# Forgetting attention on one core: the two f16 halves of every third probability tile both on GpSimd, and a scale folded into the ones column

## The chip, the cores and the metric

The kernel runs on one core of a Trainium2 chip. The metric is the device time of one execution in microseconds (us). A core has five engines that run their own queues and meet through semaphores: TensorE (PE: matrix multiply; PEld is its weight load), VectorE (DVE), ScalarE (ACT), GpSimd (POOL) and SyncE (SP), which here issues the transfers.

## The reference

One layer of a hybrid mixer over 2048 tokens of width 1024. A normalised input is projected and split over three groups of heads: a gated linear recurrence, a pooling mixer, and attention with a forget gate in 8 heads of 64. The change touches only the third:

```python
def _forgetting_attention(q, k, v, log_f):
    B, T, H, D = q.shape
    c = jnp.cumsum(log_f, axis=1).transpose(0, 2, 1)
    scale = D ** -0.5
    outs = []
    for i in range(T // Q_BLOCK):
        q0, q1 = i * Q_BLOCK, (i + 1) * Q_BLOCK
        s = jnp.einsum('bqhd,bkhd->bhqk', q[:, q0:q1], k[:, :q1]).astype(jnp.float32) * scale
        mask = (q0 + jnp.arange(Q_BLOCK))[:, None] >= jnp.arange(q1)[None, :]
        bias = jnp.where(mask, c[:, :, q0:q1, None] - c[:, :, None, :q1], 0.0)
        p = jax.nn.softmax(jnp.where(mask, s + bias, MASK_VALUE), axis=-1)
        outs.append(jnp.einsum('bhqk,bkhd->bqhd', p.astype(v.dtype), v[:, :q1]))
    return jnp.concatenate(outs, axis=1)
```

Its output is multiplied by a SiLU gate, joined with the other two groups and mapped by one output projection.

## The kernel before

**Stages.** Up to about 670 us the kernel makes all projections, the recurrence and the pooling mixer. From there to about 1170 us it runs the attention, with the gate projection (tiles pgc), then the output projection (tiles y) fed in between as filler matmuls. After that come the last output rows.

**Numbers in f16 pairs.** Every factor of a matmul is kept as a high and a low f16 half. So a probability tile is made as pf (f32), ph (its f16 rounding) and pl (pf minus ph in f16), and each value product takes three matmuls into the bank o: ph by the values' high half with a ones column beside it (65 columns), ph by the low half (64), pl by the high half and the ones column (65). The ones column gives the row sum, as column 64 of o. It is set once, by a GpSimd memset on the value tile Vt (L686).

**The attention's loops.** Queries come in 4 groups g of 512, and for each group the 8 heads h follow; a head sweeps 4g+4 key tiles j of 128. That makes 320 steps (g, h, j). A step is one call of `scores` (L1002): matmuls into a score bank st (two banks), an exponential on ScalarE into pf (L1019; three buffers), then ph and pl, by a counter k that goes 0, 1, 2 over the steps:

- k = 0: GpSimd copies pf to ph (L1021), VectorE subtracts to pl (L1024).
- k = 1: ScalarE makes ph by a second exponential (L1023), GpSimd subtracts to pl (L1024).
- k = 2: ScalarE makes ph (L1023), VectorE subtracts to pl (L1024).

`values` (L1027) issues the value products four steps later (LAG). At a head's last step VectorE takes the reciprocal of the row sums (rl, L1045), multiplies it by a constant (L1046) and scales o by it into oc (L1048). The bank o is single: the next head's first value product waits until L1048 has read it.

**Row maxima.** A third stream, `max_steps` (L956), runs ahead by about one head: TensorE makes scores into the banks mx (three), VectorE reduces each to a column of M (L979 for a full tile, L976 for one on the diagonal), and the head's maxima become Mf (L985, L986) and an f16 pair Mc (L988, L989). TensorE transposes Mc (mt, L995), and ScalarE copies it into QB (L997), without which no score of that head can be made.

**Order.** The kernel's text interleaves these streams, and a scheduler then fixes the order of the instructions on each engine when the kernel is built, from its own estimate of when each could start. At run time every engine works through its list in that order, so an instruction that has to wait holds all that stand behind it. y is drained by VectorE (L1086, L1095), with a small GpSimd power (L1091) between; a finished pair of heads is gated (L1051) and split (L409 on ScalarE, L411 on VectorE).

Of the kernel before, what the change touches and what calls it, by code (L numbers as in the profile page):

```python
# [16 lines left out]
ALU = mybir.AluOpType  # L17
# [14 lines left out]
INV = 1.0 / (SW * SH)  # L32
SM = 16.0
SV = 16.0
# [20 lines left out]
def kernel(  # L55
# [7 lines left out]
    V, S, G, PE = nc.vector, nc.scalar, nc.gpsimd, nc.tensor  # L63
# [357 lines left out]
    def store_tm(src, slot, g):  # L421
        for v, dst in zip(split(spool, src, 1.0, f"mx{slot}_{g}_"), (mh_d, ml_d)):
            nc.sync.dma_start(dst[g * GT:(g + 1) * GT, slot * P:(slot + 1) * P].rearrange("(t p) c -> p t c", p=P),
                              v.rearrange("p (t c) -> p t c", t=4))
# [258 lines left out]

    vp = ctx.enter_context(tc.tile_pool(name="vp", bufs=1, side="right", reuse_waits="tile"))
    Vt = vp.tile([P, NT, 8, 130], F16, tag="Vt", name="Vt")
    G.memset(Vt[:, :, :, 64:65], SV)  # L686

    negq = vp.tile([P, GT], BF16, tag="negq", name="negq")
    G.memset(negq, 0.0)
# [219 lines left out]
    def bank(tag, name):  # L909
        return psB.tile([P, 512], F32, tag=tag, name=name, bufs=BANKS[tag])  # L910
# [91 lines left out]
    def scores(n, g, h, j):  # L1002
        i = n % NQ
        q0 = max(0, j - 4 * g)
        off = q0 * P
        diag = j >= 4 * g
        c, jj = j // 4, j % 4
        st = bank("st", f"st{g}_{h}_{j}")
        PE.matmul(st[:, off:], K2[c][:, h, jj * P:(jj + 1) * P], QQs[i][:, off:], start=True, stop=False)  # L1009
        PE.matmul(st[:, off:], KA[c][:68, h, jj * P:(jj + 1) * P], QBs[i][:68, off:], start=False, stop=not diag)  # L1010
        if diag:
            PE.matmul(st[:, off:off + P], idb, negk, start=False, stop=True)
        pf = wk.tile([P, GT], F32, tag="pf", name=f"pf{g}_{h}_{j}", bufs=3)
        ph = wk.tile([P, GT], F16, tag="ph", name=f"ph{g}_{h}_{j}", bufs=6)
        pl = wk.tile([P, GT], F16, tag="pl", name=f"pl{g}_{h}_{j}", bufs=5)
        bias = biasg[:, g, 8 * j + h:8 * j + h + 1]
        k = state["step"] % 3
        state["step"] += 1
        S.activation(pf[:, off:], st[:, off:], AF.Exp, bias=bias, scale=0.125)  # L1019
        if k == 0:  # L1020
            G.tensor_scalar(ph[:, off:], pf[:, off:], 1.0, 1.0, op0=ALU.mult, op1=ALU.mult)  # L1021
        else:
            S.activation(ph[:, off:], st[:, off:], AF.Exp, bias=bias, scale=0.125)  # L1023
        (G if k == 1 else V).tensor_tensor(pl[:, off:], pf[:, off:], ph[:, off:], op=ALU.subtract)  # L1024
        return ph, pl, q0

    def values(n, g, h, j, ph, pl, q0):  # L1027
        if j == 0:
            state[n] = bank("o", f"o{g}_{h}")
        po = state[n]  # L1030
        pov = po[:, :260].rearrange("p (q d) -> p q d", d=65)
        for qi in range(q0, 4):
            qs = slice(qi * P, (qi + 1) * P)
            PE.matmul(pov[:, qi, :], ph[:, qs], Vt[:, j, h, 0:65], start=(j == 0 and qi == 0), stop=False, skip_group_check=True)  # L1034
            PE.matmul(pov[:, qi, 0:64], ph[:, qs], Vt[:, j, h, 65:129], start=False, stop=False, skip_group_check=True)  # L1035
            PE.matmul(pov[:, qi, :], pl[:, qs], Vt[:, j, h, 0:65], start=False, stop=(j == 4 * g + qi), skip_group_check=True)  # L1036
        if j < 4 * g + 3:
            return
        if h % 2 == 0:
            state["oc"] = wk.tile([P, 4, P], F32, tag="oc", name=f"oc{g}_{h}", bufs=2)  # L1040
            state["gt"] = wk.tile([P, 4, P], F32, tag="gt", name=f"gtl{g}_{h}", bufs=1)
            nc.sync.dma_start(state["gt"], gc_d[g * GT:(g + 1) * GT, (h // 2) * P:(h // 2 + 1) * P].rearrange("(q p) c -> p q c", p=P))
        oc, gt = state["oc"], state["gt"]
        rl = wk.tile([P, 4], F32, tag="rl", name=f"rl{g}_{h}", bufs=2)
        V.reciprocal(rl, pov[:, :, 64])  # L1045
        V.tensor_scalar(rl, rl, SM * INV * 0.5, None, op0=ALU.mult)  # L1046
        cs = slice(64 * (h % 2), 64 * (h % 2) + 64)
        V.tensor_tensor(oc[:, :, cs], pov[:, :, 0:64], rl.unsqueeze(2).to_broadcast([P, 4, 64]), op=ALU.mult)  # L1048
        del state[n]
        if h % 2 == 1:  # L1050
            V.tensor_tensor(oc, oc, gt, op=ALU.mult)  # L1051
            store_tm(oc.rearrange("p q c -> p (q c)"), 2 + h // 2, g)
# [73 lines left out]
    def pop_value():  # L1126
        a = pend.pop(0)
        values(*a)
        n, g, h, j = a[:4]
        if h == 7 and j == 4 * g + 3:  # L1130
            state["closing"] = (state["step"] + 10, g)
# [20 lines left out]
    for n, (g, h) in enumerate(order):  # L1152
        for j in range(4 * g + 4):
            while deadlines and deadlines[0] <= step:
                deadlines.pop(0)
                next(maxs, None)
            pend.append((n, g, h, j) + scores(n, g, h, j))
            if "closing" in state and state["step"] >= state["closing"][0]:
                state["done"] = state.pop("closing")[1] + 1
            credit += RATE  # L1160
            while credit > 0.0:
                cost = next(fill, None)
                if cost is None:
                    credit = 0.0
                else:
                    credit -= cost
            if len(pend) > LAG:
                pop_value()
            step += 1
# [33 lines left out]
```

## Time and profile before

| what | value |
|---|---|
| median of 3 runs | 1251.9 us (1248.07 to 1254.1) |
| the profiled execution | 1248.18 us, span 1246.4 us |
| granted TensorE clock | 0.987 |
| busy share: PE, DVE, ACT, POOL | 94%, 65%, 49%, 32% |

The span runs from the first to the last instruction; 1.8 us of the execution lie around it. Matmuls overlap in the records, so a busy TensorE is not one at its peak, but a hole in its row is a real wait. The lines that the prediction rests on stand with it.

### The profile page before, as it was taken

To read this page: it belongs to the slowest core of one execution; us is meant where nothing else is said; L and a number is where in the kernel's file an instruction comes from. 1 tells how busy PE (TensorE), PEld (TensorE's weight loads), DVE (VectorE), ACT (ScalarE), POOL (GpSimd) and SP (SyncE) were. 2 spreads that over 40 slices of the span, in tenths; PEclk is the share of its full clock that TensorE was granted. 3 is DMA by queue.
4 is the path that set the end of the run, shared out by engine and by line. 5 is a ranking of instruction groups with operands and counts; after the bars stand their busy time and mean duration, and the time that the engine had idled before them with its cause. 6 is when DMAs were issued, how large, how long until landed. Compare 5 with 4: busy or idle time off the path is not lost.

```text
span 1246.4 us, 25487 instructions
## 1 busy us (share of the span) xinstructions
PE 1170.5 (94%) x9949; PEld 749.9 (60%) x9949; DVE 812.2 (65%) x1736; ACT 609.5 (49%) x1176; POOL 403.7 (32%) x500
## 2 busy tenths in 40 slices
PE   5877999999999999999999999999989899999998
PEld 3445667655644588884447767755555555555544
DVE  5787878887433243214364799788788888888522
ACT  5756444553121222212122677667767676777611
POOL 2645555553130020002230223234334343434400
PEclk9988999999999999999999999999999999999999
DMA  9646100113175232101112343285223222321263
GB/s 226 184 115 170 44 17 18 52 35 93 43 183 142 71 107 71 35 2 43 26 51 70 89 140 110 69 178 127 67 64 85 68 78 79 65 51 38 80 162 104
DMA packets 168137, 107.56 MB, mean 86 GB/s; under 512 B 95824, under 2 KB 159568, under 8 KB 168016
## 3 DMA queue, kind: packets, MB, share of 16 engines
q1 hardware_dynamic: 166976, 105.92, 32.2%
q8 instruction: 78, 1.28, 0.4%
q14 instruction: 43, 0.35, 0.1%
q10 hardware_dynamic: 1040, 0.00, 0.0%
HBM read 59.62 MB, written 31.59 MB: 73 GB/s over the span
## 4 chain that ended last, share of the span: by engine, by line
PE 62%; DVE 19%; ACT 6%; issue 5%; POOL 4%; DMA 4%; SPq 0%; POOLq 0%; DVEq 0%; ACTq 0%
PE y L1078 11%; PE pq L183 7%; PE pv L194 6%; PE pgc L194 5%; PE pu L183 3%; PE st L1009 3%; PE st L1010 3%; PE pgb L183 3%; PE pk L183 3%; DVE pl L1024 3%; PE mx L973 3%; DVE M L979 3%; PE o L1034 2%; PE o L1035 2%; PE pf L183 2%
## 5 line engine op out<-in xcount | busy, mean ns | idle before, releaser
L1019 ACT ACTIVATE pf<-st,biasg 128x512 f32<-128x512 f32 (+1 forms) x320 | 199.6, 625 | 93.9 <-PE st L1010 53.2
L194 PEld LDWEIGHTS <-hTh 128*128 128x128 f16 x1536 | 151.0, 99 | 44.3 <-DMA hTh<-xh 16.1
L1024 DVE TENSOR_TENSOR pl<-pf,ph 128x512 f16<-128x512 f32 (+1 forms) x213 | 139.9, 658 | 42.4 <-POOL ph L1021 24.8
L1024 POOL TENSOR_TENSOR pl<-pf,ph 128x512 f16<-128x512 f32 (+2 forms) x107 | 114.2, 1067 | 147.7 <-ACT ph L1023 137.6
L979 DVE TENSOR_REDUCE M<-mx 128x1 f32<-128x512 f32 x192 | 129.2, 682 | 9.4 <-PE mx L973 8.5
L1023 ACT ACTIVATE ph<-st,biasg 128x512 f16<-128x512 f32 (+2 forms) x213 | 131.4, 617 | 2.1 <-PE o L1036 2.1
L1034 PE MATMUL o<-Vt,ph 128*128 128x65 f16 x1088 | 129.7, 193 | 2.8 <-DVE oc L1048 2.4
L1035 PE MATMUL o<-Vt,ph 128*128 128x64 f16 x1088 | 130.2, 195 | 0.0
L1036 PE MATMUL o<-Vt,pl 128*128 128x65 f16 x1088 | 129.2, 192 | 0.0
L1021 POOL TENSOR_SCALAR ph<-pf 128x512 f16<-128x512 f32 (+1 forms) x107 | 66.0, 617 | 192.4 <-ACT pf L1019 130.8
L1034 PEld LDWEIGHTS <-ph 128*128 128x128 f16 x1088 | 102.6, 96 | 34.5 <-issue 5.5
L1009 PE MATMUL st<-QQ,K 128*128 128x512 f16 (+1 forms) x320 | 111.5, 349 | 5.6 <-ACT ph L1023 5.0
L1035 PEld LDWEIGHTS <-ph 128*128 128x128 f16 x1088 | 101.8, 97 | 24.5 <-issue 1.1
L1036 PEld LDWEIGHTS <-pl 128*128 128x128 f16 x1088 | 102.3, 99 | 0.4
L1078 PE MATMUL y<-woh,mh 128*128 128x512 f16 (+2 forms) x264 | 98.2, 373 | 0.0
L1078 PE MATMUL y<-woh,ml 128*128 128x512 f16 (+2 forms) x264 | 98.0, 373 | 0.0
L1078 PE MATMUL y<-wol,mh 128*128 128x512 f16 (+2 forms) x264 | 98.0, 373 | 0.0
L973 PE MATMUL mx<-KA,QM 68*128 68x512 f16 (+1 forms) x224 | 79.5, 358 | 5.7 <-DVE M L979 4.1
L194 PEld LDWEIGHTS <-hTl 128*128 128x128 f16 x768 | 75.5, 98 | 9.9
L1010 PE MATMUL st<-QB,KA 68*128 68x512 f16 x224 | 80.1, 358 | 0.0
L1078 PEld LDWEIGHTS <-mh 128*128 128x128 f16 x528 | 49.4, 98 | 50.4 <-issue 0.7
L976 DVE CUSTOM_DVE_ANT_0 mx<-mx,negq 128x128 f32<-128x128 f32 (+3 forms) x128 | 62.3, 492 | 12.0 <-PE mx L973 11.5
(327 smaller groups left out, 2691.1 us busy)
## 6 DMA issues: line engine op xcount, KB each, us to landing
xt<-in_x_dram SPq DMA_DIRECT2D x16, 512.0 KB, 4.4
xr<-in_x_dram SPq DMA_DIRECT2D x16, 512.0 KB, 4.5
out_dram<-yt SPq DMA_DIRECT2D x15, 512.0 KB, 3.1
QQ<-qh_d SPq DMA_DIRECT2D x64, 64.0 KB, 2.3
wo<-in_w_out_dram SPq DMA_DIRECT2D x16, 256.0 KB, 3.0
gc_d<-gtc SPq DMA_DIRECT2D x32, 128.0 KB, 2.0
gtl<-gc_d SPq DMA_DIRECT2D x16, 256.0 KB, 2.9
wst_q<-in_w_in_dram SPq DMA_DIRECT2D x12, 256.0 KB, 2.9
```

Of the source, the lines that this page charges most:

```text
L183: PE.matmul(ps, a[:, k, c0:c0 + P], b[:, k, :], start=i == 0, stop=i == 3 * KC - 1)
L194: PE.matmul(ps, a[:, k, :], b[:, k, c0:c0 + n], start=i == 0, stop=i == 3 * KC - 1)
L979: V.tensor_reduce(dst, mx[:, :w], op=ALU.max, axis=AX.X)
L1009: PE.matmul(st[:, off:], K2[c][:, h, jj * P:(jj + 1) * P], QQs[i][:, off:], start=True, stop=False)
L1010: PE.matmul(st[:, off:], KA[c][:68, h, jj * P:(jj + 1) * P], QBs[i][:68, off:], start=False, stop=not diag)
L1019: S.activation(pf[:, off:], st[:, off:], AF.Exp, bias=bias, scale=0.125)
L1023: S.activation(ph[:, off:], st[:, off:], AF.Exp, bias=bias, scale=0.125)
L1024: (G if k == 1 else V).tensor_tensor(pl[:, off:], pf[:, off:], ph[:, off:], op=ALU.subtract)
L1034: PE.matmul(pov[:, qi, :], ph[:, qs], Vt[:, j, h, 0:65], start=(j == 0 and qi == 0), stop=False, skip_group_check=True)
L1035: PE.matmul(pov[:, qi, 0:64], ph[:, qs], Vt[:, j, h, 65:129], start=False, stop=False, skip_group_check=True)
L1036: PE.matmul(pov[:, qi, :], pl[:, qs], Vt[:, j, h, 0:65], start=False, stop=(j == 4 * g + qi), skip_group_check=True)
L1078: PE.matmul(py, a[:, k, :], b[:, k, cs], start=i == 0, stop=i == 3 * KC - 1)
```

## The change

At k = 0 the subtraction moves from VectorE to GpSimd, so GpSimd makes ph and then pl of the same step. At k = 1 it moves from GpSimd to VectorE. Over three steps each engine has as many instructions as before. The constant of L1046 goes: its reciprocal is now in the ones column, so the row sum comes out already scaled, and lines behind it are numbered one lower (L1048 becomes L1047, L1095 becomes L1094).

```diff
     Vt = vp.tile([P, NT, 8, 130], F16, tag="Vt", name="Vt")
-    G.memset(Vt[:, :, :, 64:65], SV)
+    G.memset(Vt[:, :, :, 64:65], SV / (SM * INV * 0.5))
...
         else:
             S.activation(ph[:, off:], st[:, off:], AF.Exp, bias=bias, scale=0.125)
-        (G if k == 1 else V).tensor_tensor(pl[:, off:], pf[:, off:], ph[:, off:], op=ALU.subtract)
+        (G if k == 0 else V).tensor_tensor(pl[:, off:], pf[:, off:], ph[:, off:], op=ALU.subtract)
         return ph, pl, q0
...
         V.reciprocal(rl, pov[:, :, 64])
-        V.tensor_scalar(rl, rl, SM * INV * 0.5, None, op0=ALU.mult)
         cs = slice(64 * (h % 2), 64 * (h % 2) + 64)
```

With other instructions to place, the scheduler also sets some others in another order. Names below are tile_head_key tile with the buffer's number behind.

VectorE in group g = 2, from the last maxima of head 5 (Mf_5) to its pair Mc_5, before:

```order
L985 TENSOR_REDUCE Mf_5_10948<-M_5_10947 128x4
L1024 TENSOR_TENSOR pl_4_6_11266<-pf_4_6_11264,ph_4_6_11265 128x512
L411 TENSOR_TENSOR mx_2_l<-oc_2_10852,mx_2_h 128x512
L986 TENSOR_SCALAR Mf_5_10948<-Mf_5_10948,cref_74 128x4
L979 TENSOR_REDUCE M_6_11289<-mx_6_0_0_11291 128x1
L988 CAST Mc_5_11258<-Mf_5_10948 128x4
L979 TENSOR_REDUCE M_6_11289<-mx_6_0_1_11315 128x1
L989 TENSOR_TENSOR Mc_5_11258<-Mf_5_10948,Mc_5_11258 128x4
```

and after:

```order
L411 TENSOR_TENSOR mx_2_l<-oc_2_10834,mx_2_h 128x512
L976 ISA mx_5_3_2_11233,M_5_10928<-mx_5_3_2_11233,negq 128x512
L976 ISA M_5_10928 128x1
L979 TENSOR_REDUCE M_6_11269<-mx_6_0_0_11271 128x1
L985 TENSOR_REDUCE Mf_5_10929<-M_5_10928 128x4
L986 TENSOR_SCALAR Mf_5_10929<-Mf_5_10929,cref_74 128x4
L988 CAST Mc_5_11238<-Mf_5_10929 128x4
L979 TENSOR_REDUCE M_6_11269<-mx_6_0_1_11295 128x1
L989 TENSOR_TENSOR Mc_5_11238<-Mf_5_10929,Mc_5_11238 128x4
```

The subtraction of step 6 (k = 0 there) has left VectorE, and nothing of the probabilities stands between L985 and L989 any more. Among the eight heads of that group a subtraction stood in this stretch in six and now stands in two; in g = 3 it stood in four and now stands in five.

VectorE at the end of head 4 of the same group, from the row sums rl to oc, before:

```order
L1045 RECIPROCAL rl_4_11531<-o_4_11213 128x4
L979 TENSOR_REDUCE M_6_11289<-mx_6_3_0_11535 128x1
L1024 TENSOR_TENSOR pl_5_3_11518<-pf_5_3_11516,ph_5_3_11517 128x512
L1046 TENSOR_SCALAR rl_4_11531<-rl_4_11531 128x4
L979 TENSOR_REDUCE M_6_11289<-mx_6_3_1_11563 128x1
L1048 TENSOR_TENSOR oc_4_11528<-o_4_11213,rl_4_11531 128x4x64
```

and after:

```order
L1045 RECIPROCAL rl_4_11511<-o_4_11193 128x4
L979 TENSOR_REDUCE M_6_11269<-mx_6_3_0_11514 128x1
L1047 TENSOR_TENSOR oc_4_11508<-o_4_11193,rl_4_11511 128x4x64
L979 TENSOR_REDUCE M_6_11269<-mx_6_3_1_11542 128x1
L1024 TENSOR_TENSOR pl_5_4_11522<-pf_5_4_11520,ph_5_4_11521 128x512
```

One reduction, and here one subtraction, no longer stand ahead of the read that frees the bank o.

TensorE at the start of head 4 of that group, up to the first value product into the bank that the head before leaves (o), before:

```order
L973 LDWEIGHTS QM_3240
L973 MATMUL mx_5_3_2_11253<-K_9289,QM_3240 128x512
L1009 LDWEIGHTS K_1_3232
L1009 MATMUL st_4_6_11261<-QQ_3239,K_1_3232 128x512
L1010 LDWEIGHTS KA_3233
L1010 MATMUL st_4_6_11261<-QB_3237,KA_3233 128x512
L1078 LDWEIGHTS mh_10347
L1078 MATMUL y_1_11114<-woh,mh_10347 128x512
L1034 LDWEIGHTS ph_4_0_11109
L1034 MATMUL o_4_11213<-Vt,ph_4_0_11109 128x65
```

and after:

```order
L1009 LDWEIGHTS K_1_3232
L1009 MATMUL st_4_5_11209<-QQ_3239,K_1_3232 128x512
L1010 LDWEIGHTS KA_3233
L1010 MATMUL st_4_5_11209<-QB_3237,KA_3233 128x512
L1077 LDWEIGHTS mh_10330
L1077 MATMUL y_1_11095<-woh,mh_10330 128x512
L1034 LDWEIGHTS ph_4_0_11090
L1034 MATMUL o_4_11193<-Vt,ph_4_0_11090 128x65
L1035 LDWEIGHTS ph_4_0_11090
L1035 MATMUL o_4_11193<-Vt,ph_4_0_11090 128x64
```

The first value product stood behind a maximum and the score matmuls of step 6; it now stands behind those of step 5. GpSimd's list keeps its alternation of a copy (L1021) and a subtraction (L1024); the subtraction is now that of the same step.

## The prediction

> **What bounds the kernel now.** I read the page's busy shares first, then the stage that the change touches, then who waits for whom there.
>
> ```profile
> PE 1170.5 (94%) x9949; PEld 749.9 (60%) x9949; DVE 812.2 (65%) x1736; ACT 609.5 (49%) x1176; POOL 403.7 (32%) x500
> ```
>
> TensorE carries the span, but these are averages over stages. The stretch from 680 to 1170 us holds nearly all of the 320 steps; its columns are busy us and instructions of PE, PEld, DVE, ACT and POOL:
>
> ```profile
> 680.00:1170.00 490.00, 465.78 (x5384) 298.57 (x5383) 413.43 (x960) 349.17 (x648) 182.04 (x219) 1.00 0.33 87
> ```
>
> TensorE has 490 - 465.8 = 24.2 us of holes there, at a granted clock of 1.00. Its matmuls aren't touched, so about 24 us, 2% of the time, is the most that any reordering of the other engines can give, and only if every hole closed. VectorE is the next fullest engine (84%). What TensorE waited for in that stretch (total us, times, longest):
>
> ```profile
> PE mx L973 <- DVE M L979: 6.1, 8, 1.8
> PE mt L995 <- DVE Mc L989: 5.9, 7, 1.2
> PE st L1009 <- ACT ph L1023: 5.0, 7, 1.5
> PE mx L973 <- DVE M L976: 2.5, 3, 2.0
> PE o L1034 <- DVE oc L1048: 2.4, 6, 0.7
> ```
>
> Most of the holes are VectorE being late: with a maximum, with the pair Mc, with oc. So the question is what the change does to VectorE's queue. Two waits of VectorE itself bear on it:
>
> ```profile
> DVE pl L1024 <- POOL ph L1021: 23.3, 37, 1.9
> DVE pl L1024 <- ACT ph L1023: 13.1, 17, 2.1
> ```
>
> How much of a microsecond on VectorE reaches the end is read from the chain of work for this stretch:
>
> ```profile
> by line: PE y L1078 14.5%; PE pgc L194 8.7%; PE st L1009 8.3%; PE st L1010 7.7%; DVE pl L1024 7.2%; PE mx L973 7.1%; DVE M L979 6.8%; PE o L1034 4.8%; PE o L1035 4.8%; PE o L1036 4.5%; issue 3.3%; DVE mx L976 2.2%; DMA wo<-in_w_out_dram 2.0
> L979 DVE TENSOR_REDUCE M<-mx 128x1 f32<-128x512 f32 x192 | 129.2, 682 | 9.4 <-PE mx L973 8.5
> ```
>
> L979 is busy 129.2 us and stands in the chain with 6.8% of 490 = 33 us. So I count a quarter of VectorE's time where I know no better.
>
> **The change part by part.** *The work itself.* The groups in the same stretch:
>
> ```profile
> L1024 DVE TENSOR_TENSOR pl<-pf,ph 128x512 f16<-128x512 f32 x147 | 110.6, 754 | 28.0 <-POOL ph L1021 16.1 <-ACT ph L1023 11.0
> L1024 POOL TENSOR_TENSOR pl<-pf,ph 128x512 f16<-128x512 f32 x74 | 89.4, 1207 | 106.5 <-ACT ph L1023 99.0 <-PE o L1036 3.4 <-PE st L1010 1.8
> L1021 POOL TENSOR_SCALAR ph<-pf 128x512 f16<-128x512 f32 x74 | 50.4, 682 | 135.3 <-ACT pf L1019 92.8 <-PE st L1010 12.4 <-PE o L1036 10.3
> L1046 DVE TENSOR_SCALAR rl<-rl 128x4 f32<-128x4 f32 x31 | 8.1, 261 | 0.0
> ```
>
> Each third subtraction stays on GpSimd, so its busy time and VectorE's stay as they are, but for L1046. GpSimd sat idle 106.5 and 135.3 us ahead of these groups, so its length costs nothing. Its slowest tile was ready 1.2 us behind ScalarE's ph of step k = 1; it will be ready 0.7 + 1.2 = 1.9 us behind pf of step k = 0. The value products come four steps later, and 490 us over 320 steps is 1.5 us a step: 6 us of cover, so 0. (Were that cover gone, each of 107 tiles would hold TensorE up to 0.7 us.) The constant in the ones column costs nothing: the memset is the same instruction, long before. No transfer is added.
>
> *The pair Mc.* One of TensorE's waits on it, VectorE's rows first, then GpSimd's and TensorE's, and last the cast's shortest, median and longest time in ns:
>
> ```profile
> 927.25 0.15 DVE L985 TENSOR_REDUCE Mf<-M 128x4 f32<-128x12 f32 x1
> 927.84 0.69 DVE L1024 TENSOR_TENSOR pl<-pf,ph 128x512 f16<-128x512 f32 x1 [0.44 <-POOL ph L1021]
> 928.45 0.68 DVE L411 TENSOR_TENSOR mx_l<-oc,mx_h 128x512 f16<-128x512 f32 x1
> 929.05 0.22 DVE L986 TENSOR_SCALAR Mf<-Mf,cref 128x4 f32<-128x4 f32 x1
> 929.79 0.83 DVE L988 CAST Mc<-Mf 128x4 f16<-128x4 f32 x1
> 931.13 0.15 DVE L989 TENSOR_TENSOR Mc<-Mf,Mc 128x4 f16<-128x4 f32 x1
> ...
> 929.44 1.15 POOL L1024 TENSOR_TENSOR pl<-pf,ph 128x512 f16<-128x512 f32 x1 [1.63 <-ACT ph L1023]
> ...
> 931.33 0.38 PE L995 MATMUL mt<-idh,Mc 128*2 128x128 f16 x4 [1.18 <-DVE Mc L989]
> ...
> L988 DVE CAST Mc<-Mf x30: 154/172/1122, 684.3 to 1148.3; 128x4 f16<-128x4 f32 x30
> ```
>
> From L985 to L989 it took 3.9 us, because a subtraction that waited for GpSimd's copy and L411 stood between, and the cast then fell on GpSimd's subtraction (0.83 us, where the median is 0.17). In the new order this stretch holds only L986, L988, one reduction and L989: 0.2 + 0.2 + 0.7 + 0.2 = 1.3 us, at worst 2.4 with a GpSimd subtraction (1.15) in the way: 1.5 to 2.6 us sooner than now, against a wait of 1.2. The group with six such heads now has two, the last group five for four. I take 4 of the 5.9 us: -4.0 (bounds 0 and -5.9).
>
> *L1046 and oc.* Six waits for oc cost 2.4 us. One of the late L1048:
>
> ```profile
> 1019.76 0.97 DVE L1046 TENSOR_SCALAR rl<-rl 128x4 f32<-128x4 f32 x1
> 1020.76 0.42 DVE L1048 TENSOR_TENSOR oc<-o,rl 128x256 f32<-128x256 f32 x1
> ...
> 1019.55 1.16 POOL L1024 TENSOR_TENSOR pl<-pf,ph 128x512 f16<-128x512 f32 x1 [1.10 <-ACT ph L1023]
> ```
>
> L1046 sat behind GpSimd's subtraction and held oc. Without it, and with one reduction fewer ahead, oc ends 0.26 + 0.68 = 0.9 us sooner in the mean. But TensorE's first value product was moved ahead past a maximum and two score matmuls, which the chain has as
>
> ```profile
> 992.26 0.22 PE mx L973
> 992.48 0.22 PE st L1009
> 992.69 0.22 PE st L1010
> ```
>
> 0.66 us, so only 0.3 us a head is left over: -1.2 (bounds -2.4 and +3.0, the latter if 0.1 us is lost at each of 31 heads).
>
> *The rest of VectorE.* It no longer waits for GpSimd's copy (23.3 us), but twice as many subtractions now wait for ScalarE, so up to another 13.1 us is to be expected: 10.2 us net, and 8.1 us of L1046, 18.3 in all; a quarter is 4.6 us. Most of that is counted under Mc and oc already: -1.5 (bounds 0 and -4.6).
>
> *Two engines side by side.* GpSimd now reads for 1.9 us at a stretch. What that does to a subtraction on VectorE is seen where one met it:
>
> ```profile
> 903.32 1.63 DVE L1095 SCALAR_TENSOR_TENSOR yt<-yt,oss,xr 128x1024 f32<-128x1024 f32 x1 [0.68 <-POOL oss L1091]
> 904.88 1.63 DVE L1024 TENSOR_TENSOR pl<-pf,ph 128x512 f16<-128x512 f32 x1
> ...
> 904.58 1.38 POOL L1024 TENSOR_TENSOR pl<-pf,ph 128x512 f16<-128x512 f32 x1 [0.70 <-ACT ph L1023]
> ```
>
> GpSimd began 0.3 us earlier and ended at 905.96; VectorE, coming late from L1095, ended at 906.51, 0.55 later: it had waited out the whole of the other's run, where 0.69 is usual. Until now step 1's subtraction was the one on GpSimd, and VectorE's two were clear of it. Now VectorE's step 1 comes against GpSimd's step 0. Whether they meet depends on ScalarE's pace, here a tight triple and a wide one:
>
> ```profile
> 1069.79 0.62 POOL L1021 TENSOR_SCALAR ph<-pf 128x512 f16<-128x512 f32 x1 [1.17 <-PE st L1010]
> 1070.41 0.68 ACT L1023 ACTIVATE ph<-st,biasg 128x512 f16<-128x512 f32 x1
> ...
> 996.10 0.62 POOL L1021 TENSOR_SCALAR ph<-pf 128x512 f16<-128x512 f32 x1 [0.58 <-ACT pf L1019]
> 997.31 0.68 ACT L1023 ACTIVATE ph<-st,biasg 128x512 f16<-128x512 f32 x1
> ```
>
> GpSimd would end its subtraction 0.62 + 1.16 = 1.78 us behind its copy's start at the soonest: at 1071.57 and at 997.88. ScalarE's ph is there at 1071.09 and 997.99. So 0.5 us of waiting in the tight case, none in the wide one. ScalarE is 71% busy (349 of 490 us); I take half of 107 triples as tight, and VectorE there in time for half of those: 107 x 0.25 x 0.5 = 13 us, less about half of the 147 x (0.754 - 0.69) = 9 us that meetings cost today: +8.5 on VectorE, +2.0 on the end (bounds -1 and +13, the latter if all 107 wait 0.5 us).
>
> The Trainium skill, page "SBUF — State Buffer", section "Who interferes with whom", speaks against this change: a VectorE instruction with two SBUF inputs contends with a GpSimd instruction that reads SBUF, and whoever starts first keeps the shared read port for its whole instruction. The trace agrees (1.63 us for 0.69). By that rule the term is +2.0 as it stands, and the first rival below is the case where it strikes in every triple; were the port shared evenly instead, a meeting would cost half, and the term would be (6.5 - 4.5) x 0.25 = +0.5.
>
> Sum: -4.0 - 1.2 - 1.5 + 2.0 = -4.7 us. Against the profiled execution (1248.2) that is 1243.5; the median of the runs stands 3.7 us above that execution, so I forecast 1247.2.
>
> **The rivals.** *The subtractions collide (slower).* At every triple VectorE's step 1 waits for GpSimd's step 0, with the reductions behind it. Price: 107 x 0.5 = 53 us on VectorE, 13 on the end; less 6.7 of gains: 1258. For it: the 0.5 us of the tight triple, and that VectorE was held for the whole of GpSimd's run. Against: in the wide triple there is nothing to wait for, and VectorE waited for ScalarE's ph only 17 times so far, so mostly it comes to a subtraction late. It decides from 27 / 107 = 0.25 us a triple (a quarter of 27 us is the 6.7).
>
> *Nothing moves.* The other holes take the place: a maximum late behind L1095, or ScalarE late with st (5.0 us), which the change does not touch. For it: mx and st are 13.6 of the 21.9 us listed above. Then 0 to -2 us: 1251.
>
> *All of VectorE's waits go.* If the 23.3 us are not replaced by waits for ScalarE, and Mc and oc are never late: -5.9 - 2.4 - 4.6 = -13 us: 1239. Against it: the list still has seven heads with a subtraction in the way of Mc.
>
> **How the numbers follow.** About 0.5% (6.3 us) is what a measurement of this kernel can tell from no change. My forecast's case, -3 to -9 us (1243 to 1249), has 0.47, of it 0.20 beyond 0.5%; the large gain 0.15; nothing moves 0.18, with 0.02 beyond on each side; the collisions 0.20, of it 0.18 beyond. Faster: 0.20 + 0.15 + 0.02 = 0.37; slower: 0.18 + 0.02 = 0.20; same: 0.43. The range reaches to the large gain and to just short of the collisions: 1238 to 1257.
>
> **What would show it.** In the new profile the wait of L1024 on VectorE for GpSimd must be gone and that for ScalarE be 13 to 26 us; TensorE's wait of mt for Mc about 2 us (5.9 before); GpSimd's subtraction must follow its copy with no idle time; VectorE's 512-wide L1024 has a mean of 0.75 to 0.85 us. A mean above 0.9 would be the collisions. The prediction is wrong if TensorE's holes in this stretch, 24 us, grow, or shrink by more than 10.

## The result and the profile after

| kernel | median of its runs | range |
|---|---|---|
| before | 1250.7 us (4 runs) | 1248.1 to 1254.1 |
| changed | 1241.4 us (4 runs) | 1239.6 to 1243.0 |

The ratio is 0.9931 (95% interval 0.991 to 0.9952): 8.6 us faster by the ratio, with 6.0 to 11.3 for its interval. The forecast was a gain of 4.7 us, 1247. The sign and the range held, and the gain is nearly twice the forecast. The profiled execution took 1239.62 us, 8.6 less than the one of before. Its busy shares, from the page:

```profile
PE 1167.9 (94%) x9949; PEld 750.2 (61%) x9949; DVE 811.0 (66%) x1704; ACT 608.3 (49%) x1176; POOL 407.7 (33%) x500
```

VectorE's busy time is only 1.2 us lower (812.2 before), although L1046 with its 8.3 us over the whole span is gone: something else on VectorE became longer by 7 us. The stretch from 680 to 1170 us, in the same columns as before:

```profile
680.00:1170.00 490.00, 473.13 (x5518) 305.34 (x5517) 415.76 (x936) 354.30 (x659) 189.15 (x223) 1.00 0.33 87
```

TensorE's holes went from 24.2 to 16.9 us, so this stage holds nearly all of the gain. What TensorE waited for there (total us, times, longest):

```profile
PE o L1034 <- DVE oc L1047: 6.2, 7, 2.1
PE st L1009 <- ACT ph L1023: 5.3, 9, 1.4
PE mx L973 <- DVE M L979: 2.7, 3, 2.0
PE mt L995 <- DVE Mc L989: 1.7, 5, 0.5
```

Against the list of before: mt fell from 5.9 to 1.7, the maxima (all rows with mx) from 9.6 to 2.7, and oc rose from 2.4 to 6.2. All of TensorE's waits in the stretch together went from 23.3 to 15.9 us. A small rest is the clock: before, it was granted at 0.94 from 1040 to 1070 us (the column ahead of the last two), about 1.8 us, and after it was not. Before, then after:

```profile
1040.00:1070.00 30.00, 27.86 (x293) 15.81 (x290) 25.15 (x52) 20.34 (x37) 11.09 (x14) 0.94 0.29 80
```

```profile
1040.00:1070.00 30.00, 29.66 (x352) 17.67 (x351) 26.49 (x53) 22.05 (x39) 14.07 (x15) 1.00 0.25 72
```

VectorE's own wait, and the groups of the subtraction on both engines:

```profile
DVE pl L1024 <- ACT ph L1023: 30.8, 46, 2.4
```

```profile
L1024 DVE TENSOR_TENSOR pl<-pf,ph 128x512 f16<-128x512 f32 x149 | 109.6, 736 | 24.9 <-ACT ph L1023 23.3 <-issue 0.5
L1024 POOL TENSOR_TENSOR pl<-pf,ph 128x512 f16<-128x512 f32 x75 | 92.1, 1228 | 6.1
L1024 DVE TENSOR_TENSOR pl<-pf,ph 128x256 f16<-128x256 f32 x24 | 15.4, 643 | 4.7 <-ACT ph L1023 4.4
```

The wait for GpSimd's copy is gone and the one for ScalarE has more than doubled. The 512-wide subtraction is no dearer than before (754), and GpSimd's follows its copy with hardly any idle time.

### The profile page after: what moved, and what is told of

The parts are those of the page before. It is cut to its first block, busy times and chain, and to the rows that moved or that the text cites. A ratio compares the mean times of both kernels' runs of the same rounds, so it can differ in the third digit from the quotient of the medians.

```text
span 1237.8 us, 25511 instructions
## 1 busy us (share of the span) xinstructions
PE 1167.9 (94%) x9949; PEld 750.2 (61%) x9949; DVE 811.0 (66%) x1704; ACT 608.3 (49%) x1176; POOL 407.7 (33%) x500
## 3 DMA queue, kind: packets, MB, share of 16 engines
q10 hardware_dynamic: 1040, 0.00, 0.0%
## 4 chain that ended last, share of the span: by engine, by line
PE 63%; DVE 18%; ACT 6%; issue 5%; DMA 4%; POOL 3%; SPq 0%; POOLq 0%; DVEq 0%; ACTq 0%
PE y L1077 11%; PE pq L183 7%; PE pv L194 6%; PE pgc L194 6%; PE st L1009 4%; PE pu L183 3%; PE st L1010 3%; PE mx L973 3%; PE pgb L183 3%; PE pk L183 3%; PE o L1035 2%; PE o L1034 2%; DVE pl L1024 2%; PE o L1036 2%; DVE M L979 2%
## 5 line engine op out<-in xcount | busy, mean ns | idle before, releaser
L1021 POOL TENSOR_SCALAR ph<-pf 128x512 f16<-128x512 f32 (+1 forms) x107 | 67.3, 629 | 315.5 <-ACT pf L1019 235.9
L1024 DVE TENSOR_TENSOR pl<-pf,ph 128x512 f16<-128x512 f32 (+2 forms) x213 | 142.9, 673 | 33.6 <-ACT ph L1023 30.8
L979 DVE TENSOR_REDUCE M<-mx 128x1 f32<-128x512 f32 x192 | 129.4, 682 | 6.9 <-PE mx L973 6.4
L1024 POOL TENSOR_TENSOR pl<-pf,ph 128x512 f16<-128x512 f32 (+1 forms) x107 | 116.2, 1086 | 9.7 <-POOL ph L1021 1.0
L194 PE MATMUL pgc<-wh_gc,hTh 128*128 128x256 f16 x256 | 68.7, 279 | 1.2 <-DVE gtb L859 1.2
```

What stands on the lines that cost most here:

```text
L194: PE.matmul(ps, a[:, k, :], b[:, k, c0:c0 + n], start=i == 0, stop=i == 3 * KC - 1)
L979: V.tensor_reduce(dst, mx[:, :w], op=ALU.max, axis=AX.X)
L1024: (G if k == 0 else V).tensor_tensor(pl[:, off:], pf[:, off:], ph[:, off:], op=ALU.subtract)
```

## The experiments

All are compared with runs of the kernel before on the same chip. The columns mt, mx and o add up TensorE's waits for that bank between 680 and 1170 us, whatever released it; the sum counts every row of that list. Where the text sets a run against the changed kernel, it takes the 1241.4 us of above; the kernel before had medians of 1250.5 to 1251.7 us beside the several runs, so such a difference is good to about 1 us.

| kernel | ratio to before (95%) | us against before | mt | mx | o | sum of waits |
|---|---|---|---|---|---|---|
| before | | | 5.9 | 9.6 | 2.6 | 23.3 |
| changed | 0.9931 (0.991 to 0.9952) | -8.6 | 1.7 | 2.7 | 6.2 | 15.9 |
| subtraction moved only | 0.9958 (0.9943 to 0.9973) | -5.3 | 2.6 | 5.5 | 7.0 | 19.6 |
| constant folded only | 0.9988 (0.9972 to 1.0003) | -1.5 | 8.2 | 7.4 | 1.4 | 21.5 |
| GpSimd subtracts at k = 2, folded | 1.0001 (0.999 to 1.0012) | +0.1 | 9.0 | 4.1 | 7.9 | 25.2 |
| before, Mc first | 0.9965 (0.9952 to 0.9977) | -4.4 | 3.4 | 9.2 | 2.4 | 19.6 |
| before, maxima first | 1.0097 (1.0082 to 1.0112) | +12.1 | 9.0 | 3.2 | 7.8 | 24.9 |
| changed, oc first | 0.9932 (0.9919 to 0.9946) | -8.5 | 3.7 | 3.8 | 4.2 | 17.2 |
| changed, oc and Mc first | 0.9942 (0.9928 to 0.9955) | -7.3 | 3.2 | 4.8 | 4.0 | 17.7 |
| changed, two banks o | 0.9926 (0.9911 to 0.9941) | -9.3 | 1.8 | 9.9 | 0 | 15.7 |

**Which part carries the gain: the moved subtraction alone.**

```diff
-        (G if k == 1 else V).tensor_tensor(pl[:, off:], pf[:, off:], ph[:, off:], op=ALU.subtract)
+        (G if k == 0 else V).tensor_tensor(pl[:, off:], pf[:, off:], ph[:, off:], op=ALU.subtract)
```

> The kernel before with the subtraction alone moved (GpSimd at k = 0, VectorE at k = 1); the multiply by the constant and the old ones column stay. Placement theory: the gain hangs on the new places of the subtractions, through the pair Mc and the maxima, so this alone is 6 to 9 us faster than before (ratio .993 to .995), with TensorE's wait of mt for Mc about 2 us, of mx for M about 3 us, and of o for oc about 2.4 us as before. Fold theory: the gain comes from the 8 us of VectorE that L1046 took, so this is 0 to 3 us faster (ratio .998 to 1.000), with mt near 6 and mx near 9 us.

It is 5.3 us faster (3.4 to 7.1). TensorE's waits:

```profile
PE o L1034 <- DVE oc L1048: 7.0, 8, 2.0
PE mx L973 <- DVE M L979: 5.3, 6, 2.0
PE st L1009 <- ACT ph L1023: 4.1, 7, 1.6
PE mt L995 <- DVE Mc L989: 2.6, 5, 0.9
```

The greater part of the gain hangs on the move, as the placement theory said, though a little less than its 6 to 9. Two of its figures were wrong: 7.0 us for oc where 2.4 were expected, and 5.5 for the maxima where it had 3. With the fold alone (next) TensorE's first value product also stands ahead at most heads, and TensorE waits 1.4 us. So it is the move that makes oc late, not the value product put ahead by itself.

**The fold alone.**

```diff
-        (G if k == 0 else V).tensor_tensor(pl[:, off:], pf[:, off:], ph[:, off:], op=ALU.subtract)
+        (G if k == 1 else V).tensor_tensor(pl[:, off:], pf[:, off:], ph[:, off:], op=ALU.subtract)
```

(against the changed kernel)

> The changed kernel with the subtractions put back where they were (GpSimd at k = 1): only the constant in the ones column is left of the change. Placement theory: 0 to 3 us faster than before, TensorE's waits of mt about 6 and of mx about 9 us as before, and that of o for oc 4 to 6 us, since TensorE's first value product is moved ahead with VectorE's oc. Fold theory: 6 to 9 us faster (ratio .993 to .995).

1.5 us faster, and the interval (3.5 faster to 0.4 slower) reaches no change. The fold theory is out. TensorE's waits, from one of its longer executions (1253.4 us, where its median is 1249.1):

```profile
PE mt L995 <- DVE Mc L989: 8.2, 7, 2.1
...
PE o L1034 <- DVE oc L1047: 1.4, 3, 0.8
```

The fold did what the prediction gave it, a shorter way to oc: 1.4 us of waiting, where before had 2.4 and the expectation 4 to 6. VectorE's busy times over the span add up: fold alone 806.8, move alone 816.4, both 811.0, before 812.2. With or without the other, the fold takes 5.4 us from VectorE and the move adds 4.2; with the 2.9 us by which the fold stays behind L1046's 8.3, that is the 7 us noted above. The two gains add up to 6.8 us; the measured 8.6 lies within their intervals, so nothing more between the two is shown.

**GpSimd's subtraction at k = 2.**

```diff
-        (G if k == 0 else V).tensor_tensor(pl[:, off:], pf[:, off:], ph[:, off:], op=ALU.subtract)
+        (G if k == 2 else V).tensor_tensor(pl[:, off:], pf[:, off:], ph[:, off:], op=ALU.subtract)
```

> The changed kernel with GpSimd's subtraction at k = 2 and VectorE's at k = 0 and 1; the work of each engine is that of the changed kernel. Placement theory: VectorE waits for GpSimd's copy again (over 15 us in all between 680 and 1170 us), and the time is that of the fold alone within 3 us, 0 to 4 us faster than before. Rival, that any new order of the lists shakes the holes loose: 5 to 9 us faster than before although that wait is there.

No change (1.3 us faster to 1.5 slower), and VectorE waits for GpSimd's copy more than ever:

```profile
DVE pl L1024 <- POOL ph L1021: 37.0, 54, 2.4
```

So this new order of the lists is no gain, and the rival falls as far as one other order can show it. What sets this kernel apart from the changed one is that VectorE takes steps whose ph GpSimd makes, while in the changed one it takes none.

**The pair Mc by itself.** Only VectorE's list differs from before, and only at five heads of g = 2.

```diff
-            if g > 0:
-                V.tensor_reduce(Mf, M[:, :, :g + 1], op=ALU.max, axis=AX.X)
...
+            with tc.high_priority():
+                if g > 0:
+                    V.tensor_reduce(Mf, M[:, :, :g + 1], op=ALU.max, axis=AX.X)
...
```

(the four instructions up to Mc stand under it)

> The kernel before with only the pair Mc moved: the four small VectorE instructions from the head's maxima to Mc get high priority, so no subtraction stands between them; the lists of TensorE, ScalarE and GpSimd are those of before. If the prediction's term for Mc is right by itself: TensorE's wait of mt for Mc falls from 5.9 to 2 us or less and the time is 3 to 5 us below before (ratio .996 to .9975). Rival, that such a gain is swallowed by the next wait: mt falls as well, but the time is within 1.5 us of before.

4.4 us faster (2.9 to 6.0), with nothing of the change in it. TensorE waits less for Mc, and the rest of its list stays (the inserted line shifts numbers by one):

```profile
PE mx L973 <- DVE M L979: 5.7, 7, 1.8
...
PE mt L996 <- DVE Mc L990: 3.4, 5, 1.1
```

But the edit did not do what the expectation says of it: at each of these heads two subtractions stand between the maxima and Mc, where before had one. This is the head that the prediction showed:

```profile
927.94 0.15 DVE L986 TENSOR_REDUCE Mf<-M 128x4 f32<-128x12 f32 x1
928.02 0.68 DVE L1025 TENSOR_TENSOR pl<-pf,ph 128x512 f16<-128x512 f32 x1
928.62 0.58 DVE L987 TENSOR_SCALAR Mf<-Mf,cref 128x4 f32<-128x4 f32 x1
929.10 0.68 DVE L411 TENSOR_TENSOR mx_l<-oc,mx_h 128x512 f16<-128x512 f32 x1
929.70 0.16 DVE L989 CAST Mc<-Mf 128x4 f16<-128x4 f32 x1
929.77 0.68 DVE L1025 TENSOR_TENSOR pl<-pf,ph 128x512 f16<-128x512 f32 x1
930.37 0.15 DVE L990 TENSOR_TENSOR Mc<-Mf,Mc 128x4 f16<-128x4 f32 x1
```

From the maxima to the end of Mc it took 2.6 us instead of 4.0: the first subtraction no longer waits there for GpSimd's copy, the cast no longer falls on GpSimd's subtraction, and two reductions are out of the way. At two other heads the same way is shorter too (2.6 us for 3.6 and 4.0), and at these three TensorE's waits of 0.7 to 1.2 us are gone; at the two that are left it is longer. So an earlier Mc does end the wait, and the time fell by what the prediction's term says. But the wait fell by 2.5 us only (to 3.4, not to 2), and all waits together by 3.7. Its executions also had a slightly higher granted clock, 0.988 in the mean against 0.986 before. That the time came to the term's size is in part luck, and the run does not show what subtractions out of the way are worth.

**The maxima first.** The kernel before with the reductions of L976 and L979 under high priority.

```diff
+                    with tc.high_priority():
                         if last:
                             V.tensor_tensor_reduce(mx[:, :w], mx[:, :w], negq[:, GT - w:], 1.0, -3e38,
...
```

> The kernel before with the reductions of the maxima (L976, L979) given high priority, nothing else; the scheduler then also moves some of TensorE's matmuls. If TensorE's waits of mx for M (9.6 us before, 2.7 in the changed kernel) are worth what they show: they fall to 3 us or less and the time is 4 to 7 us below before. Rival, that the holes re-form elsewhere (at oc, or the pair Mc): within 2 us of before.

The waits for maxima did fall, to 3.2 us, and the kernel became 12.1 us slower (10.3 to 14.0):

```profile
PE mt L996 <- DVE Mc L990: 9.0, 10, 1.6
PE o L1035 <- DVE oc L1049: 6.8, 11, 2.2
```

Mc and oc took their place, so the rival was right about the holes, but not about the time. TensorE's waits grew by 1.6 us only. Most of the loss goes with the clock, which was granted lower in two stretches than in any other (1.00 before in both):

```profile
830.00:860.00 30.00, 28.16 (x281) 14.87 (x280) 20.59 (x57) 17.58 (x34) 9.21 (x11) 0.83 0.73 160
...
1100.00:1170.00 70.00, 64.54 (x736) 37.92 (x735) 54.77 (x111) 46.50 (x86) 26.58 (x32) 0.95 0.19 46
```

By an estimate that is 30 x 0.17 + 70 x 0.05 = 8.6 us. Why less was granted stays open.

**oc first, and both first.** The changed kernel, with the reciprocal and L1047 under high priority; then also the pair Mc.

```diff
-        V.reciprocal(rl, pov[:, :, 64])
...
-        V.tensor_tensor(oc[:, :, cs], pov[:, :, 0:64], rl.unsqueeze(2).to_broadcast([P, 4, 64]), op=ALU.mult)
+        with tc.high_priority():
+            V.reciprocal(rl, pov[:, :, 64])
+            V.tensor_tensor(oc[:, :, cs], pov[:, :, 0:64], rl.unsqueeze(2).to_broadcast([P, 4, 64]), op=ALU.mult)
```

> The changed kernel with the reciprocal and the scaling into oc given high priority by the scheduler, so that no drain of y and no subtraction stands between them on VectorE; some of TensorE's first value products move ahead with it. If the 6.2 us that TensorE waits for oc in the changed kernel come from what stands between: that wait falls to 2 us or less and the time is 3 to 5 us below the changed kernel (1236 to 1238). Rival, that TensorE then waits for the next thing, a maximum or the pair Mc: the waits' sum stays and the time is within 1.5 us of the changed kernel.

> The changed kernel with both given high priority, the pair Mc and the scaling into oc. If the waits add up: 4 to 7 us below the changed kernel (1234 to 1237). Rival, that the sum of the waits stays: within 2 us of it.

Neither is faster than the changed kernel: 1243.0 us with oc first and 1243.7 with both, against 1241.4. High priority cleared the drain of y from the way to oc, but not every subtraction: at 1111.6 us, for one, a subtraction still stands between the reciprocal and oc. With both, the instructions from the maxima to Mc stand in groups 2 and 3 as they do in the changed kernel, so that run adds little. With oc first:

```profile
PE st L1009 <- ACT ph L1023: 5.5, 8, 1.0
PE mt L995 <- DVE Mc L989: 3.7, 7, 1.4
PE o L1034 <- DVE oc L1048: 3.5, 4, 2.1
PE mx L973 <- DVE M L979: 3.5, 3, 2.0
```

The 2 us taken from oc came back at Mc and the maxima: the rival's sum of waits held, or rose a little (17.2 and 17.7 us for 15.9).

**Two banks for o.** The changed kernel with `BANKS = dict(mx=2, st=2, o=2, ty=2)`, where it has 3, 2, 1, 2.

> The changed kernel with two banks for o and two for the maxima instead of one and three. If the 6.2 us that TensorE waits for oc come from the single bank, that wait goes to 0. Whether the time falls depends on what two banks for the maxima cost: if nothing, 4 to 6 us below the changed kernel; rival, that TensorE then waits for maxima (over 10 us on mx, against 2.7): 5 us or more above it.

```profile
PE mx L973 <- DVE M L979: 7.2, 9, 1.7
PE st L1009 <- ACT ph L1023: 4.0, 8, 1.5
PE mx L973 <- DVE M L976: 2.5, 4, 0.9
```

The wait for oc vanished, and 7.2 us more were waited for maxima. The time is that of the changed kernel (1241.1 and 1241.4), so neither theory's time came out. The sum, 15.7 us for 15.9, did not move. None of the kernels tried is measurably faster than the changed one.

**What a meeting with GpSimd costs.** The changed kernel with GpSimd's subtraction issued twice:

```diff
+        if k == 0:
+            G.tensor_tensor(pl[:, off:], pf[:, off:], ph[:, off:], op=ALU.subtract)
```

> The changed kernel with GpSimd's subtraction at k = 0 issued twice (the same tile written again), so that GpSimd reads SBUF for about 1.15 us longer in each of 107 steps; the lists of TensorE and ScalarE are the same and VectorE's nearly so. If meetings of the two engines cost as the prediction sized them (0.5 us on VectorE where they meet, a quarter of it at the end): VectorE's 512-wide subtraction has a mean of 0.9 us or more and the time is 5 to 13 us above the changed kernel. Rival, that VectorE comes late enough and has slack enough to hide them: within 2 us of the changed kernel.

1282.2 us, 40.8 above the changed kernel, three times the most that was expected. GpSimd is busy 131.8 us more (539.5 in all), VectorE 48.5 more (859.5), and TensorE waits 42 us in the stage. The groups (the doubled one is L1026):

```profile
L1024 DVE TENSOR_TENSOR pl<-pf,ph 128x512 f16<-128x512 f32 x134 | 125.0, 935 | 11.7 <-ACT ph L1023 11.0
...
L1026 POOL TENSOR_TENSOR pl<-pf,ph 128x512 f16<-128x512 f32 x68 | 90.0, 1323 | 5.2
```

Is it the reading, or that GpSimd is busy? A first try put memsets of a scratch tile behind the subtraction:

```diff
+        if k == 0:
+            scr = wk.tile([P, P], F16, tag="scr", name=f"scr{g}_{h}_{j}", bufs=1)
+            for _ in range(5 - q0):
+                G.memset(scr, 0.0)
```

> The changed kernel with GpSimd kept busy about 1.1 us longer behind its subtraction at k = 0 as in the run with the subtraction issued twice, but by memsets of a scratch tile, which read nothing (five of 128x128 for a full tile). The lists of TensorE, VectorE and ScalarE are those of the changed kernel. If the 41 us of the doubled subtraction came from GpSimd reading SBUF beside VectorE: VectorE's 512-wide subtraction keeps its mean of about 0.74 us, and the time is within 4 us of the changed kernel. Rival, that GpSimd being busy for longer is what costs (its next copy and its small powers come later): more than 20 us above the changed kernel.

1269.2 us, but it tells nothing of the question. Nothing ties the scratch tile to its step, and the scheduler put the memsets early and in lumps: 133 of the 477 ran ahead of the attention's first copy (not all, as the next expectation has it), the others in lots of some 20 between the copies that follow, the last at 792 us. Between 680 and 800 us:

```profile
L1028 POOL MEMSET scr<- 128x128 f16 x369 | 75.3, 204 | 19.5
```

```profile
ACT pf L1019 <- POOL pl L1024: 43.4, 16, 5.3
```

ScalarE waited there 43 us for GpSimd to free buffers. The second try wrote over pf, which ties each memset to its step:

```diff
+        if k == 0:
+            G.memset(pf[:, off:], 0.0)
+            G.memset(pf[:, off:], 1.0)
```

> The changed kernel with two memsets on GpSimd behind its subtraction at k = 0, over the same step's pf, which nobody reads any more: GpSimd is busy about 1.05 us longer in each of 107 steps, and pf's buffer is freed as late as with the doubled subtraction, but nothing is read. (In the run with memsets of a scratch tile the scheduler had put all of them ahead of the attention's first copy, so they fell on the stage from 690 to 800 us in a lump.) The lists of TensorE, VectorE and ScalarE are those of the changed kernel but for one place. If the 41 us of the doubled subtraction came from GpSimd reading SBUF beside VectorE: VectorE's 512-wide subtraction keeps its mean of 0.74 us and the time is within 5 us of the changed kernel. Rival, that GpSimd being busy and pf coming free later is what costs: 20 to 40 us above the changed kernel, with that mean unchanged. Third, that memsets hold VectorE up as reads do: a mean of 0.9 us and 20 to 40 us.

1242.4 us, 1.0 above the changed kernel and within the spread of both. GpSimd was busy 504.4 us against 407.7, and VectorE's subtraction kept its mean:

```profile
L1024 DVE TENSOR_TENSOR pl<-pf,ph 128x512 f16<-128x512 f32 x149 | 109.8, 738 | 24.1 <-ACT ph L1023 21.4 <-PE st L1012 1.7 <-PE o L1039 0.2
...
L1026 POOL MEMSET pf<- 128x512 f32 x75 | 39.3, 525 | 4.3
```

So GpSimd has room for 1 us more a step. Of the 42 us that TensorE waited with the doubled subtraction, 4.2 were for GpSimd's pl itself, which that run makes later; most of the loss came from GpSimd's reading beside VectorE. The Trainium skill, page "SBUF — State Buffer", section "Who interferes with whom", says that a VectorE instruction with two SBUF inputs contends with a GpSimd one that reads SBUF, not with one that only writes it; both runs agree (935 and 738 ns). Writing was not free for every instruction: the cast L988 took 340 ns in the mean beside the memsets, and 231 in the changed kernel.

**What a microsecond of VectorE costs.** The changed kernel with VectorE's subtraction at k = 2 issued twice:

```diff
+        if k == 2:
+            V.tensor_tensor(pl[:, off:], pf[:, off:], ph[:, off:], op=ALU.subtract)
```

> The changed kernel with VectorE's subtraction at k = 2 issued twice (the same tile written again): 106 x about 0.65 us, some 65 us more of VectorE in the attention stage, away from GpSimd's subtraction. By the prediction's conversion (a quarter of a VectorE microsecond reaches the end): 16 us above the changed kernel. Rival, that VectorE has little slack left once its waits are used up, as the doubled GpSimd subtraction suggests (48.5 us more on VectorE, 41 us at the end): 40 to 65 us above it.

1271.7 us, 30.3 above the changed kernel, between the two theories. VectorE was busy 63.0 us more:

```profile
PE 1174.6 (93%) x9949; PEld 750.9 (59%) x9949; DVE 874.0 (69%) x1810; ACT 609.7 (48%) x1176; POOL 427.7 (34%) x500
```

That is 0.48 us at the end for each us on VectorE, though here the scheduler also moved some of TensorE's matmuls, so it is no pure price. With the doubled GpSimd subtraction it was 40.8 / 48.5 = 0.84, and with the fold alone 1.5 / 5.4 = 0.28, an imprecise one.

## Why the prediction was right, and where it was not

*The pair Mc* (-4.0): right in size and cause. TensorE's wait fell by 4.2 us. At the six heads where it had waited over 0.7 us, the way from the maxima (L985) to the end of Mc (L989) took 2.7 to 4.0 us before and 1.5 to 2.2 after, as the prediction had it (1.3 to 2.4); with the move alone it took 2.0 to 2.5, with the fold alone 2.7 to 3.7.

*L1046 and oc* (-1.2): right for the fold alone, where the wait went from 2.4 to 1.4 us, but wrong for the change: it rose to 6.2. The place that the prediction chose to show (head 4 of g = 2) is one where the new list is shorter. It did not look at where the drain of y (L1094) and a subtraction that now meets GpSimd's stand ahead of oc. Such a place in the changed kernel, VectorE and then GpSimd:

```profile
1108.76 1.63 DVE L1094 SCALAR_TENSOR_TENSOR yt<-yt,oss,xr 128x1024 f32<-128x1024 f32 x1
1110.32 1.64 DVE L1024 TENSOR_TENSOR pl<-pf,ph 128x512 f16<-128x512 f32 x1
1111.88 0.41 DVE L1047 TENSOR_TENSOR oc<-o,rl 128x256 f32<-128x256 f32 x1
...
1109.41 2.00 POOL L1024 TENSOR_TENSOR pl<-pf,ph 128x512 f16<-128x512 f32 x1
```

GpSimd is held by L1094 (2.00 us for 1.16), then VectorE by GpSimd (1.64 for 0.69), and oc behind both; TensorE waited 1.1 us there. The other waits for oc are not all of this kind: the longest, 2.1 us at 941 us, follows a subtraction beside GpSimd's (1.26 us) with no drain, one of 1.3 us at 870 follows a drain with no subtraction.

*The maxima* had no term of their own, and this is the step that failed. Only the rival "nothing moves" spoke of them, and it kept them as they were; the one term that could hold them, *the rest of VectorE* (-1.5), had -4.6 as its bound. They gave the largest share of the waits that went, from 9.6 to 2.7 us. The prediction had one of their places in its hands: the meeting at 903.32 to 906.51, which it quoted for its price, stands ahead of a maximum for which TensorE then waited (before):

```profile
907.10 0.38 PE L973 MATMUL mx<-K,QM 68*128 68x512 f16 x1 [2.01 <-DVE M L976]
```

L1095, then the subtraction of step 0 held by GpSimd's of step 1, then the maximum. Three more such places, at 870, 977 and 1053 us, made waits of about 1.5 to 1.8 us; with this one that is 6.7 of the 9.6 us. In the changed kernel one is left, where GpSimd's copy is what the subtraction meets:

```profile
974.40 0.38 PE L973 MATMUL mx<-KA,QM 68*128 68x512 f16 x1 [1.99 <-DVE M L979]
```

So the meetings of before were priced by VectorE's average (half of 9 us saved, a quarter of that), while four of them stood on TensorE's path. That the maxima come sooner because those meetings are gone is read from these rows; no run changed the meetings alone, and with the maxima first the same waits went without any gain.

*Two engines side by side* (+2.0): the sum took 8.5 us more on VectorE; the move added 4.2 (816.4 - 812.2). VectorE's step 1 mostly comes after GpSimd's step 0 is done: the 512-wide mean came to 736 ns, 14 below the forecast 0.75 to 0.85 us. The 256-wide one went from 432 to 643. The rival of collisions did not come true; its price was also wrong. At the rate of the doubled subtraction, 53 us of such waiting would not cost 13 us but some 45, by an estimate (53 x 0.84).

*The quarter* was taken from the chain's share of one line. It fits a small saving (0.28 with the fold) and fails for additions of 50 to 60 us (0.48 and 0.84), perhaps because VectorE's own idle time is used up. Why the two differ is not settled; with the doubled GpSimd subtraction pl also came later, and with VectorE's the lists changed.

*VectorE's waits*: that for GpSimd went from 23.3 to 0 as forecast. That for ScalarE became 30.8, above the 13 to 26 expected, presumably because VectorE is no longer held by the copy and comes sooner to steps that ScalarE has not finished.

In the sum, by TensorE's waits, Mc was right, oc was off by 5 us the wrong way, the unforeseen maxima were worth 6.9, and the rest (clock and start of the stage) about 1. The two misses largely cancel, so that the time lies as near the forecast as it does is in part luck.

## What to carry to other kernels

Where a full engine works through a fixed list and its consumer waits now for this, now for that result, add up all waits of the consumer: giving one result priority, or a second bank, moved the holes to another (oc first, two banks, maxima first), while the move that took a cause of lateness out of the list made the sum smaller. It is no rule: Mc first made the sum smaller too, by 3.7 us. And read in the new list whether a priority cleared what it was meant to clear; for Mc it did not. Here it paid to give GpSimd both halves of a step, so that VectorE waits for GpSimd in none. Count what GpSimd reads beside VectorE, not how long it is busy: 97 us more of memsets cost 1 us here or nothing, 132 us more with reading cost 41. When a row shows a meeting, look also at who waits behind it.

## What was not expected of the hardware

A meeting passes on: GpSimd's subtraction, held by L1094, took 2.00 us for 1.16 and then held VectorE's for 1.64 instead of 0.69. And the smallest instructions can pay as much as the large ones: L986, four elements a partition, has a mean of 453 ns in the changed kernel (333 before). Of its 30 runs in the stage, the 14 clear of GpSimd's copies and subtractions took 0.22 us, the 16 beside one 0.65 in the mean and up to 1.17.

```profile
L986 DVE TENSOR_SCALAR Mf<-Mf,cref 128x4 f32<-128x4 f32 x30 | 13.6, 453 | 0.5
```
